# A two-layer encoder on one core: layer 0's up projection by Strassen's scheme, its first two products beside the top-k, index scores moved into the query projection

## The chip, the core and the metric

The kernel runs on one core of a Trainium2 chip. TensorE multiplies, VectorE, ScalarE and GpSimd do the elementwise work, and SyncE's queue issues all the DMAs. The metric is device time in microseconds (us) of one execution; the time before is the median of three runs. The profiler traced one more execution, and all rows here come from that one.

## What is computed

The input is 1024 tokens of width 1024, in float32. Cut to what matters:

```python
def reference(x, ...):                 # DEPTH = 2, x: (1, 1024, 1024)
    for i in range(DEPTH):
        h = rms_norm(x, norm_mix_g[i])
        x = x + (dsa_mixer(h, ...) if i == 0 else retention_mixer(h, ...))
        x = x + conv_ffn(rms_norm(x, norm_ffn_g[i]), f_w_up[i], f_conv_w[i], f_conv_b[i], f_w_down[i])

def dsa_mixer(h, w_in, q_g, k_g, iq_g, ik_g, w_out):    # 8 heads of 128, 8 index heads of 64
    ...                                # blocks of 128 queries
    rel = jax.nn.relu(jnp.einsum('bqhd,bsd->bqhs', qib, ki))
    score = jnp.einsum('bqhs,bqh->bqs', rel, wb)
    score = jnp.where(admissible[None], score, -jnp.inf)
    _, idx = lax.top_k(score, 256)     # attention over these keys only
    ...

def conv_ffn(h, w_up, conv_w, conv_b, w_down):          # D_FF = 2816
    u = h @ w_up                       # (1024, 5632)
    up = jnp.pad(u, ((0, 0), (2, 0), (0, 0)))
    u = sum(up[:, j:j + seq] * conv_w[j] for j in range(3)) + conv_b
    a, b = u[..., :D_FF], u[..., D_FF:]
    return (jax.nn.silu(a) * b) @ w_down
```

## The kernel before

Activations lie with the features on the partitions; tokens go in two halves of 512. Each float32 product is made as three products of a high and a low part (`mm3`, L137 to L139; `product`, L809, in Strassen's scheme). For every weight tile a DMA fetches `wraw`, ScalarE rounds it to `whi`, and VectorE or GpSimd subtracts to get `wlo` (`wprep`, L103); `plan_weights` lists the weights in order and says which `wlo` GpSimd makes.

Layer 0 goes like this. `in_proj` makes queries, keys and index queries of one token half. `indexer` makes the index scores of a query block: TensorE matmuls, ScalarE's relu, VectorE's weighted sum over heads (L397, L399). `topk` finds, for several blocks at once, the 256th largest score by a search over the 31 bits of a threshold: in each round VectorE counts the scores above the threshold, block by block (L420), and sets a bit by three small operations (L430 to L432); behind the last round it makes the mask, by a scan over the scores that equal the threshold (L434 to L443). `attention` goes block by block: logits, masking on VectorE (L501), exponential on ScalarE, scaling, transposes on TensorE (L529), product with the values. `out_proj` adds to `x` and sums the squares for the next norm (`square_sum`, L188), which `mean_square` (L194) adds up on TensorE.

The generators of these functions are interleaved by hand in `run`. Blocks 2 and 3 have their top-k beside `in_proj(1)`; then the attention of blocks 0 to 3 goes with the index scores of blocks 4 to 7, and their top-k, `steps(7)` a chunk, beside `ffn_half` of half 0: 22 chunks of 128 gate channels with 48 up matmuls each (two weight tiles by 24), `conv` on ScalarE and VectorE (L555 to L567), gating, and the down projection in groups of six chunks. Attention of blocks 4 to 7, `out_proj(1)`, layer 1's `retention(0)`, `ffn_half` of half 1 and `retention(1)` follow.

Layer 1's FFN (`ffn_whole`) is made for all 1024 tokens by Strassen's scheme: seven products of 12 matmuls of 512 columns stand in for the eight of a conventional 2 x 2 blocking. `B11` and `B21` are split from the first token half, `T1` to `T4` and `B22` need both halves. `ud` in DRAM takes the convolved outputs, `gate` loads them (`gin`), multiplies and splits, and the down projection works in groups of chunks listed in `DOWN`.

A scheduler with a model of the engines sets the final order of instructions on each engine; each engine then works in that order.

## Time and profile before

| what | us |
|---|---|
| median of three runs (2809.32 to 2809.56) | 2809.42 |
| the profiled execution | 2808.24 |
| its span, from first to last instruction | 2806.4 |
| TensorE busy | 2697.8 |
| VectorE busy | 1872.5 |
| ScalarE busy | 1110.8 |
| GpSimd busy | 379.7 |

The span is what the trace covers; the execution's own time lies 1.84 us above it. Busy times are sums over the span, in which several engines work at once, so an engine's share says nothing of which one is waited for in a given stretch.

### The profile page before, as it was taken

What the parts mean: (1) busy time and instruction counts of PE and PEld (TensorE: products, weight loads), DVE (VectorE), ACT (ScalarE), POOL (GpSimd) and SP (SyncE); (2) the same over time, 40 slices, a digit from 0 to 9 for tenths busy, and PEclk for the clock granted to TensorE, in tenths of its full rate; (3) what the DMA queues carried; (4) which work ended last, traced back from release to release, by engine and by line L of the source; (5) the groups of instructions that cost most, each with busy time, mean ns of one, the idle gap of its engine ahead of it and who ended that gap; (6) DMA issues with size and microseconds to landing.
All of it is one profiled execution on the core that took longest, in us unless ns stands there. A gap on an engine that the chain in (4) does not pass through costs nothing.

```text
span 2806.4 us, 31988 instructions
## 1 busy us (share of the span) xinstructions
PE 2697.8 (96%) x12152; PEld 2211.7 (79%) x12152; DVE 1872.5 (67%) x3028; ACT 1110.8 (40%) x1620; POOL 379.7 (14%) x247
## 2 busy tenths in 40 slices
PE   8987998998999999999999999999998999999999
PEld 6765776776887888888888888888886888888887
DVE  5798899999585444444767656445447977777632
ACT  6536533323464333334433334333333644544210
POOL 2555334343440000000000000000000000000000
PEclk9998999999999999999999999999999999999999
DMA  5221122222211222222332323222222322337612
GB/s 192 80 85 38 53 75 90 75 91 72 94 38 59 89 85 76 90 90 86 117 98 90 102 83 111 75 89 96 71 82 90 134 107 112 113 111 280 237 59 87
DMA packets 88170, 273.84 MB, mean 98 GB/s; under 512 B 9936, under 2 KB 11344, under 8 KB 88016
## 3 DMA queue, kind: packets, MB, share of 16 engines
q1 hardware_dynamic: 88016, 271.80, 28.7%
q8 instruction: 95, 1.56, 0.2%
q14 instruction: 59, 0.48, 0.1%
HBM read 234.54 MB, written 33.55 MB: 96 GB/s over the span
## 4 chain that ended last, share of the span: by engine, by line
PE 71%; DVE 9%; issue 2%; DMA 2%; POOL 1%; ACT 1%; SPq 0%; POOLq 0%; ACTq 0%; DVEq 0%
PE bank L137 19%; PE bank L139 19%; PE bank L138 19%; PE bank L809 13%; DVE scratch L420 3%; POOL wlo L103 1%; DVE t L561 1%; DMA gin<-ud 1%; DVE t L560 1%; PE bank L529 1%; DMA wraw<-in_wf_up 1%; DVE t L555 1%; DVE gl L584 0%; PE bank L766 0%; DMA wraw<-in_wf_dn 0%
## 5 line engine op out<-in xcount | busy, mean ns | idle before, releaser
L101 ACT ACTIVATE whi<-wraw 128x1024 fp32r<-128x1024 f32 (+3 forms) x324 | 324.5, 1003 | 676.6 <-PE bank L138 392.7
L137 PE MATMUL bank<-hh,whi 128*128 128x512 f32 (+2 forms) x1184 | 464.9, 393 | 17.9 <-ACT hh L148 11.6
L139 PE MATMUL bank<-hh,wlo 128*128 128x512 f32 (+2 forms) x1184 | 462.2, 391 | 11.0 <-POOL wlo L103 11.0
L138 PE MATMUL bank<-hl,whi 128*128 128x512 f32 (+2 forms) x1184 | 461.5, 390 | 3.5 <-DVE hl L149 3.4
L103 DVE TENSOR_TENSOR wlo<-wraw,whi 128x1024 fp32r<-128x1024 f32 (+3 forms) x227 | 266.6, 1175 | 240.8 <-ACT whi L101 238.0
L137 PEld LDWEIGHTS bank<-hh,whi 128*128 128x128 f32 (+1 forms) x1184 | 224.3, 189 | 67.2 <-ACT hh L148 13.2
L139 PEld LDWEIGHTS bank<-hh,wlo 128*128 128x128 f32 (+1 forms) x1184 | 224.0, 189 | 63.9 <-POOL wlo L103 16.1
L138 PEld LDWEIGHTS bank<-hl,whi 128*128 128x128 f32 (+1 forms) x1184 | 224.5, 190 | 51.8 <-DVE hl L149 4.3
L103 POOL TENSOR_TENSOR wlo<-wraw,whi 128x1024 fp32r<-128x1024 f32 (+2 forms) x97 | 220.0, 2271 | 309.7 <-ACT whi L101 298.7
L809 PE MATMUL bank<-T,whi 128*128 128x512 f32 x704 | 220.0, 394 | 10.4 <-ACT T L786 8.0
L138 PE MATMUL bank<-wlo,hh 128*128 128x512 f32 x512 | 199.3, 389 | 0.0
L139 PE MATMUL bank<-whi,hl 128*128 128x512 f32 x512 | 199.2, 389 | 0.0
L137 PE MATMUL bank<-whi,hh 128*128 128x512 f32 x512 | 198.8, 390 | 0.0
L420 DVE TENSOR_SCALAR_CACHE_REDUCE scratch<-sc,tkt 128x640 f16<-128x640 f32 (+1 forms) x192 | 180.5, 940 | 1.9
L786 ACT ACTIVATE whi<-wraw 128x1024 fp32r<-128x1024 f32 (+2 forms) x98 | 95.4, 973 | 198.7 <-PE bank L138 127.5
L809 PEld LDWEIGHTS bank<-T,whi 128*128 128x128 f32 x704 | 133.3, 189 | 41.2 <-ACT T L786 9.3
L809 PE MATMUL bank<-B,whi 128*128 128x512 f32 x528 | 162.8, 389 | 0.0
L787 DVE TENSOR_TENSOR wlo<-wraw,whi 128x1024 fp32r<-128x1024 f32 (+2 forms) x98 | 109.1, 1113 | 75.5 <-ACT whi L786 75.4
L139 PE MATMUL bank<-gh,wlo 128*128 128x512 f32 x352 | 139.7, 399 | 14.2 <-POOL wlo L103 13.9
L137 PE MATMUL bank<-gh,whi 128*128 128x512 f32 x352 | 138.5, 395 | 5.6 <-ACT whi L101 5.6
L138 PE MATMUL bank<-gl,whi 128*128 128x512 f32 x352 | 138.5, 394 | 0.0
L809 PE MATMUL bank<-T,wlo 128*128 128x512 f32 x352 | 137.5, 392 | 0.0
(251 smaller groups left out, 5376.9 us busy)
## 6 DMA issues: line engine op xcount, KB each, us to landing
wraw<-in_wf_up SPq DMA_DIRECT2D x135, 512.0 KB, 3.3
wraw<-in_wb_vg SPq DMA_DIRECT2D x64, 512.0 KB, 3.3
wraw<-in_wf_dn SPq DMA_DIRECT2D x72, 384.0 KB, 3.1
ud<-cu SPq DMA_DIRECT2D x44, 512.0 KB, 2.6
gin<-ud SPq DMA_DIRECT2D x44, 512.0 KB, 4.7
wraw<-in_wb_qk SPq DMA_DIRECT2D x32, 512.0 KB, 3.3
wraw<-in_wb_out SPq DMA_DIRECT2D x32, 512.0 KB, 3.3
wraw<-in_wa_in SPq DMA_DIRECT2D x26, 512.0 KB, 3.6
```

The costliest lines, as they stand in the source:

```text
L101: nc.scalar.activation(hi[:, :n], raw[:, :n], AF.Copy)
L103: eng.tensor_tensor(lo[:, :n], raw[:, :n], hi[:, :n].bitcast(F32), ALU.subtract)
L137: mm(ps, ah, bh, start=first, stop=False)
L138: mm(ps, ah, bl, start=False, stop=False)
L139: mm(ps, al, bh, start=False, stop=last)
L420: V.tensor_scalar(scratch[:, 0, :Ls[b]], scs[b], of(b), None, op0=op, op1=ALU.add, accum_out=cnt[:, b:b + 1])
L529: nc.tensor.transpose(pt[:, i * 128:(i + 1) * 128], lg[:, i, j * 128:(j + 1) * 128], self.ident)
L555: nc.vector.tensor_tensor(pn, ps, rbc, ALU.mult)
L560: nc.vector.scalar_tensor_tensor(u[:, 1:], ps[:, :511], w(1), u[:, 1:], op0=ALU.mult, op1=ALU.add)
L786: return (self.nc.scalar.activation(hi, raw, AF.Copy), self.nc.vector.tensor_tensor(lo, raw, hi.bitcast(F32), ALU.subtract))
L787: self.nc.vector.tensor_tensor(lo, raw, hi.bitcast(F32), ALU.subtract))
L809: self.nc.tensor.matmul(ps, u, v, start=first and k + i == 0, stop=k == 3 and i == 2, skip_group_check=not (first and last))
```

## The change

Layer 0's FFN is now made like layer 1's, for all tokens at once by Strassen's scheme. Two of the seven products, `A11 B11` and `A12 B21`, need the first token half alone: `first_products` makes them for 17 of the 22 chunks behind `out_proj(0)` and its norm, with three top-k steps at each of its yields, and stores them in DRAM (`pd`). The last five chunks follow `out_proj(1)`. `ffn_first` loads them and makes the five other products; for chunks from the fifth on, half of the conv is postponed to `gate` in `down`. The down projection is `down(0)`, with groups of 4, 6, 6 and 6 chunks, and `retention(0)` takes its split inputs from the last group.

The index scores of blocks 4 to 7 move into the query projection of `in_proj(1)` (`IDX_FROM`), the attention of blocks 0 to 3 goes with the start of the top-k of blocks 4 to 7, and so does `out_proj(0)` (`steps(5)` for each tile). The `halo` handling of the conv between token halves falls away, and buffers are laid out anew.

```diff
-DOWN = [(0, 6), (6, 6), (12, 6), (18, 4)]
-PRE = 4
+DOWN = (([(0, 4), (4, 6), (10, 6), (16, 6)], (14,)), ([(0, 6), (6, 6), (12, 6), (18, 4)], (0, 12)))
+PRE = (5, 4)
...
+            elif ph == "up":
+                seq += [(i["wf_up"][0, c], 1024, True) for c in range(*a)]
...
+    def first_products(self, cs, B):
+        def out(ps, c, i):
+            t = self.tmp()
+            nc.scalar.activation(t, ps, AF.Copy)
+            nc.sync.dma_start(self.pd[i][c], t)
+        last = None
+        for c in list(cs) + [None]:
+            cur = None
+            if c is not None:
+                hi, lo = self.weight()
+                a = self.bank()
+                self.product(a, (hi[:, :512], lo[:, :512]), B[0], True, False)
+                out(a, c, 0)
+                cur = c, a, (hi[:, 512:], lo[:, 512:])
+                yield
+            if last:
+                self.product(last[1], last[2], B[1], False, True)
+                out(last[1], last[0], 1)
+                yield
+            last = cur
...
+    def ffn_first(self, x, tt, s3):
+        chunk = self.normaliser(x1, C_GFFN, 1)
+        late = lambda c: c >= DOWN[0][0][0][1]
+        nxt = self.prep_b(0, 0, self.up_raw(0, 0), s3)
+        T1, T2, T4, B22, T3 = self.second_inputs(x0, x1, tt, chunk)
...
+        for c in range(NFF):
+            s1, s2, s3_, s4, a22 = nxt
...
+            nc.sync.dma_start(p1, self.pd[0][c])
+            nc.sync.dma_start(ca[:, :512], self.pd[1][c])
+            d = self.bank()
+            self.product(d, s1, T1, True, False)
+            p5 = self.tmp()
+            add(p5, d, p1)
+            if held:
+                finish(held)
+            a = self.bank()
+            self.product(a, s2, T2, True, False)
+            u2 = self.tmp()
+            add(u2, a, p1)
+            self.product(d, s4, B22, False, True)
+            add(ca[:, 512:], d, u2)
+            if c + 1 < NFF:
+                own = self.hp.tile([128, 2, 1024], F32R, tag="h", name="wb")
+                nxt = self.prep_b(0, c + 1, self.up_raw(0, c + 1), s3, (own[:, 0], own[:, 1]))
+            self.product(a, s3_, T3, False, False)
+            add(cb[:, 512:], a, p5)
+            held = c, a, a22, p1, cc
+        finish(held)
+        return self.down(0, tt, late)
...
         def gate(c):
...
+            nc.sync.dma_start(u, self.ud[l][1][c])
+            if late(c):
+                self.conv(l, NFF + c, u, v)
+                nc.sync.dma_start(u, self.ud[l][0][c])
+            else:
+                nc.sync.dma_start(v, self.ud[l][0][c])
+            add(u, u, v, ALU.mult)
...
     def run(self):
-                gens.append(self.topk([masks[2], masks[3]]))
-                att = self.attention(range(4), q0, masks, get_ot)
-                q1, qs1 = self.in_proj(1, *h1[:2], steps, lambda j, q: next(att) if j >= EARLY else None)
-                steps(100)
-                idx = (None for b in (4, 5, 6, 7) for _ in self.indexer(b, qs1, (b - 4) * 128, masks))
...
-                for i, _ in enumerate(att):
-                    if i % IDX_EVERY != 0:
-                        next(idx, None)
-                x[0] = self.out_proj(0, *ot, lambda: [next(idx, None) for _ in range(3)])
...
-                self.ffn_half(0, 0, x[0], self.ffn_part(0, 0, x[0], lag=2), steps=steps, early=early)
...
+                gens.append(self.topk([masks[2], masks[3]], scratch))
+                idx = []
+                def index(j, q, qs):
+                    if j == IDX_FROM:
+                        idx.append((None for b in (4, 5, 6, 7) for _ in self.indexer(b, qs, (b - 4) * 128, masks)))
+                    if j >= IDX_FROM:
+                        for _ in range(-(-32 // (8 - IDX_FROM))):
+                            next(idx[0], None)
+                q1, qs1 = self.in_proj(1, *h1[:2], steps, index)
+                steps(200)
+                gens.append(self.topk([masks[b] for b in (4, 5, 6, 7)], scratch))
+                for _ in self.attention(range(4), q0, masks, get_ot):
+                    steps(1)
+                x[0] = self.out_proj(0, *ot, lambda m: steps(5))
...
+                for _ in self.first_products(range(NFF - PRE[0]), B):
+                    steps(3)
+                steps(200)
+                for _ in self.attention(range(4, 8), q1, masks, get_ot):
+                    pass
+                B, ch = self.first_inputs(x[0])
+                x[1] = self.out_proj(1, *ot, lambda m: next(ch, None))
+                for i, _ in enumerate(self.first_products(range(NFF - PRE[0], NFF), B)):
+                    if i == 2:
+                        self.mean_square(1)
...
+                x, h = self.ffn_first(x, tt, s3)
```

What the scheduler makes of it on VectorE is seen at three places. The first is the attention of blocks 0 to 3; before, the rows of index scores of the later blocks (`sc<-...,wr`) stand among its masking (`lg<-bank,sc`) and scaling steps:

```order
L397 TENSOR_SCALAR sc<-t_2343,wr 128x512
L491 RECIPROCAL s_2312<-s_2297 128x1
L501 ISA lg_2091,s_2319<-bank,sc 128x384
L501 ISA s_2319 128x1
L397 TENSOR_SCALAR sc<-t_2349,wr 128x256
L506 SCALAR_TENSOR_TENSOR s_2321<-s_2319,sq 128x1
L491 RECIPROCAL s_2325<-s_2310 128x1
L491 RECIPROCAL s_2337<-s_2323 128x1
L501 ISA lg_2091,s_2374<-bank,sc 128x384
L501 ISA s_2374 128x1
```

After the change, counts of the top-k of blocks 4 to 7 (L405 now) stand there, with its small steps (`tkb`, `tkt`, `tks`) between them:

```order
L405 TENSOR_SCALAR scratch,tkc<-sc,tkt 128x896
L474 RECIPROCAL s_2485<-s_2470 128x1
L484 ISA lg_2375,s_2492<-bank,m_277 128x256
L484 ISA s_2492 128x1
L405 TENSOR_SCALAR scratch,tkc<-sc,tkt 128x1024
L489 SCALAR_TENSOR_TENSOR s_2494<-s_2492,sq 128x1
L415 TENSOR_SCALAR tkb<-tkc 128x4
L474 RECIPROCAL s_2498<-s_2483 128x1
L416 SCALAR_TENSOR_TENSOR tkt<-tkb,tks 128x4
L417 TENSOR_TENSOR tks<-tks,tkb 128x4
L405 TENSOR_SCALAR scratch,tkc<-sc,tkt 128x640
```

The scores have gone ahead of this place and about two thirds of the counting rounds have come to it and to `out_proj(0)` behind it. The second place is the top-k of blocks 4 to 7 at its middle; before, each count has conv steps of the FFN (`t<-...`) beside it:

```order
L420 TENSOR_SCALAR scratch,tkc<-sc,tkt 128x640
L560 SCALAR_TENSOR_TENSOR t_3734<-t_3732,cols,t_3734 128x511
L420 TENSOR_SCALAR scratch,tkc<-sc,tkt 128x768
L561 SCALAR_TENSOR_TENSOR t_3734<-t_3732,cols,t_3734 128x510
L555 TENSOR_TENSOR t_3740<-bank,rbc 128x512
L420 TENSOR_SCALAR scratch,tkc<-sc,tkt 128x896
L564 COPY halo<-t_3740 128x2
L560 SCALAR_TENSOR_TENSOR t_3742<-t_3740,cols,t_3742 128x511
L420 TENSOR_SCALAR scratch,tkc<-sc,tkt 128x1024
L561 SCALAR_TENSOR_TENSOR t_3742<-t_3740,cols,t_3742 128x510
L430 TENSOR_SCALAR tkb<-tkc 128x4
```

After, from the last split of `B21` on, VectorE has nothing but the top-k to the end of its 32 rounds:

```order
L405 TENSOR_SCALAR scratch,tkc<-sc,tkt 128x640
L405 TENSOR_SCALAR scratch,tkc<-sc,tkt 128x768
L405 TENSOR_SCALAR scratch,tkc<-sc,tkt 128x896
L405 TENSOR_SCALAR scratch,tkc<-sc,tkt 128x1024
L415 TENSOR_SCALAR tkb<-tkc 128x4
L416 SCALAR_TENSOR_TENSOR tkt<-tkb,tks 128x4
L417 TENSOR_TENSOR tks<-tks,tkb 128x4
L405 TENSOR_SCALAR scratch,tkc<-sc,tkt 128x640
L405 TENSOR_SCALAR scratch,tkc<-sc,tkt 128x768
L405 TENSOR_SCALAR scratch,tkc<-sc,tkt 128x896
L405 TENSOR_SCALAR scratch,tkc<-sc,tkt 128x1024
```

The conv steps are gone from beside it. The third place is the up projection of layer 0; before, here for the second token half, a chunk is conv steps of 512 columns, the gating (`t<-t,t`, `gl`) and two splits of weights:

```order
L555 TENSOR_TENSOR t_10915<-bank,rbc 128x512
L197 TENSOR_SCALAR msq<-bank 128x4
L103 TENSOR_TENSOR wlo<-wraw,whi 128x1024
L560 SCALAR_TENSOR_TENSOR t_10917<-t_10915,cols,t_10917 128x511
L561 SCALAR_TENSOR_TENSOR t_10917<-t_10915,cols,t_10917 128x510
L566 SCALAR_TENSOR_TENSOR t_10917<-halo,cols,t_10917 128x2
L567 SCALAR_TENSOR_TENSOR t_10917<-halo,cols,t_10917 128x1
L581 TENSOR_TENSOR t_10917<-t_10908,t_10917 128x512
L584 TENSOR_TENSOR gl<-t_10917,gh 128x512
L555 TENSOR_TENSOR t_10988<-bank,rbc 128x512
L103 TENSOR_TENSOR wlo<-wraw,whi 128x1024
```

After, one chunk of `ffn_first` is sums of weights (`wraw`, `t<-wraw`), sums of products from the banks, three splits and two conv steps over all tokens:

```order
L742 TENSOR_TENSOR t_7093<-wraw 128x512
L742 TENSOR_TENSOR wraw<-wraw 128x512
L742 TENSOR_TENSOR t_7039<-bank,t_7023 128x512
L742 TENSOR_TENSOR wraw<-wraw 128x512 x2
L742 TENSOR_TENSOR cu<-bank,t_6925 128x512
L742 TENSOR_TENSOR t_7073<-bank,t_7023 128x512
L709 TENSOR_TENSOR wlo<-wraw,whi 128x1024
L709 TENSOR_TENSOR wb<-wraw,wb 128x1024
L742 TENSOR_TENSOR cu<-bank,t_7073 128x512
L742 TENSOR_TENSOR cu<-bank,t_7039 128x512
L835 SCALAR_TENSOR_TENSOR cu<-cu,cols 128x1023
L709 TENSOR_TENSOR wlo_7105<-t_7093,whi_7104 128x512
L836 SCALAR_TENSOR_TENSOR cu<-cu,cols 128x1022
```

The multiplication of the two halves of the gate has moved from here to the down projection.

## Rows read from the trace of the kernel before

**Rows 1.** The page, part 1: busy us (share of span) xinstructions of each engine.

```profile
PE 2697.8 (96%) x12152; PEld 2211.7 (79%) x12152; DVE 1872.5 (67%) x3028; ACT 1110.8 (40%) x1620; POOL 379.7 (14%) x247
```

**Rows 2.** Stretches: length; busy (xinstructions) of PE, PEld, DVE, ACT, POOL; clock, DMA.

```profile
106.20:341.20 235.00, 199.48 (x908) 157.81 (x907) 210.32 (x495) 121.30 (x240) 113.22 (x75) 0.93 0.21 64
...
365.50:690.00 324.50, 294.15 (x1247) 233.04 (x1245) 321.52 (x554) 107.50 (x137) 129.25 (x55) 0.99 0.26 82
...
762.40:918.10 155.70, 148.49 (x767) 123.92 (x766) 109.63 (x272) 86.55 (x147) 34.66 (x32) 0.98 0.17 58
918.10:1351.80 433.70, 431.98 (x1985) 359.81 (x1984) 206.40 (x306) 149.72 (x233) 10.63 (x17) 1.00 0.27 90
...
2148.00:2192.70 44.70, 34.29 (x130) 25.48 (x129) 42.65 (x54) 24.00 (x30) 0.00 (x0) 0.85 0.17 59
2192.70:2545.00 352.30, 352.29 (x1555) 291.69 (x1555) 268.29 (x307) 178.07 (x209) 0.00 (x0) 1.00 0.32 117
```

**Rows 3.** Waits of the engines in 106.2 to 690: us, times, longest.

```profile
DVE x L546 <- PE bank L139: 7.5, 2, 5.7
...
PE bank L391 <- DVE s L501: 6.8, 1, 6.8
```

**Rows 4.** VectorE by line and shape, 340 to 690: xcount, busy us, mean ns.

```profile
L420 DVE TENSOR_SCALAR_CACHE_REDUCE scratch<-sc,tkt 128x1024 f16<-128x1024 f32 x32 | 40.7, 1271 | 0.3
...
L420 DVE TENSOR_SCALAR_CACHE_REDUCE scratch<-sc,tkt 128x640 f16<-128x640 f32 x32 | 27.9, 873 | 0.0
...
L430 DVE TENSOR_SCALAR tkb<-tkc 128x4 int32<-128x4 f32 x31 | 13.9, 450 | 0.3
...
L431 DVE SCALAR_TENSOR_TENSOR tkt<-tkb,tks 128x4 int32<-128x4 int32 x31 | 7.1, 229 | 0.4
L432 DVE TENSOR_TENSOR tks<-tks,tkb 128x4 int32<-128x4 int32 x31 | 6.0, 195 | 0.5
...
L434 DVE TENSOR_SCALAR tkn<-tkc 128x4 f32<-128x4 f32 x1 | 2.4, 2354 | 0.0
...
L438 DVE TENSOR_TENSOR_SCAN scratch<-scratch 128x1024 f16<-128x1024 f16 x1 | 2.3, 2275 | 0.0
```

**Rows 5.** Timeline of VectorE: start us, length us, one instruction a row.

```profile
111.25 1.97 DVE L430 TENSOR_SCALAR tkb<-tkc 128x2 int32<-128x2 f32 x1
...
116.01 0.17 DVE L430 TENSOR_SCALAR tkb<-tkc 128x2 int32<-128x2 f32 x1
...
361.29 0.87 DVE L420 TENSOR_SCALAR_CACHE_REDUCE scratch<-sc,tkt 128x640 f16<-128x640 f32 x1
...
365.77 0.17 DVE L430 TENSOR_SCALAR tkb<-tkc 128x4 int32<-128x4 f32 x1
...
560.51 0.68 DVE L555 TENSOR_TENSOR t<-bank,rbc 128x512 f32<-128x512 f32 x1
561.11 0.15 DVE L432 TENSOR_TENSOR tks<-tks,tkb 128x4 int32<-128x4 int32 x1
```

**Rows 6.** TensorE's timeline: attention of blocks 4 to 7; retention 1.

```profile
762.42 0.60 PE L529 MATMUL bank<-kon,lg 128*128 128x128 f32 x4
...
1708.16 1.16 PE L194 MATMUL bank<-ones,acc 128*128 128x128 f32 x8 [0.23 <-DVE acc L188]
```

**Rows 7.** Timeline of TensorE at layer 1's first product with T.

```profile
2155.62 0.80 PE L809 MATMUL bank<-T,whi 128*128 128x512 f32 x1 [6.27 <-ACT T L786]
```

**Rows 8.** VectorE by line and shape, 2192.7 to 2545 (layer 1's up products).

```profile
L787 DVE TENSOR_TENSOR wlo<-wraw,whi 128x1024 fp32r<-128x1024 f32 x57 | 69.7, 1223 | 70.0 <-ACT whi L786 70.0
L821 DVE TENSOR_TENSOR cu<-bank,t 128x512 f32<-128x512 f32 x76 | 50.4, 685 | 11.0 <-PE bank L809 11.0
L911 DVE SCALAR_TENSOR_TENSOR cu<-cu,cols 128x1023 f32<-128x1023 f32 x39 | 49.9, 1280 | 0.0
```

**Rows 9.** DMA traffic, 2545 to 2600 (layer 1's up projection ends).

```profile
DMA packets 6472, 18.74 MB, mean 341 GB/s; under 512 B 719, under 2 KB 719, under 8 KB 6468
```

**Rows 10.** GpSimd by line and shape, 106 to 690.

```profile
L103 POOL TENSOR_TENSOR wlo<-wraw,whi 128x1024 fp32r<-128x1024 f32 x59 | 148.2, 2513 | 208.1 <-ACT whi L101 204.6 <-PE bank L392 3.4
```

More of the change, by code (lines that the diff above doesn't have):

```diff
@@ L50 @@
 LAG = 3
-EARLY = 4
-IDX_EVERY = 2
-IDX_FIRST = 4
+IDX_FROM = 3
 class Prog:
@@ L345, in in_proj @@
             pq = self.proj_T(hh, hl)
+            steps((2, 6)[half])
+            also(j, q, qs)
             sq = squares(pq)
@@ new lines, in first_inputs, with chunks @@
+    def first_inputs(self, x0):
+        B = [self.hp.tile([128, 2, 4, 512], F32R, tag="h", name=n) for n in ("B11", "B21")]
+        def chunks():
+            for t, o in zip(B, (0, 4)):
+                for k in (0, 2):
+                    self.split(self.two(t, 0, k), self.two(t, 1, k), self.two(x0, o + k))
+                    yield
+        return B, chunks()
+    def first_products(self, cs, B):
+        nc = self.nc
+        def out(ps, c, i):
[15 more added lines that the diff above has]
+                out(last[1], last[0], 1)
+                yield
+            last = cur
@@ L887, in ffn_whole, with second_inputs @@
+    def second_inputs(self, x0, x1, tt, chunk):
+        two, add = self.two, self.add
+        T1, T2, T4, B22, T3 = [tt.tile([128, 2, 4, 512], F32R, tag="T", name=n) for n in ("T1", "T2", "T4", "B22", "T3")]
         for k in (0, 2):
@@ new lines, in run @@
+                steps(200)
[3 more added lines that the diff above has]
+                x[0] = self.out_proj(0, *ot, lambda m: steps(5))
+                ot.clear()
+                self.mean_square(0)
+                chunk = self.normaliser(x[0], C_GFFN, 0)
+                for k in range(8):
+                    chunk(k)
+                B, ch = self.first_inputs(x[0])
```

407 lines of the change are left out of this document (188 added, 219 removed).

## The prediction

> **What bounds the kernel now.** I read the page first. TensorE is busy 96% of the span and VectorE 67% [rows 1]. These are averages, so the table of stretches comes next [rows 2]. From 762.4 us to the end TensorE hardly rests: in 2192.7 to 2545 it is busy 352.29 of 352.30 us with 1555 matmuls, which gives 0.2266 us for each, at a granted clock of 1.00 (the 2.4 GHz level). Removing matmuls there shortens the run one for one. From 106.2 to 690 it is otherwise: VectorE is busy 210.32 of 235.00 us to 341.2 and 321.52 of 324.50 us from 365.5, TensorE 199.48 and 294.15. Here both are nearly full at once: the top-k of blocks 4 to 7 lies beside 325 us of TensorE's FFN matmuls. What leaves that stage on TensorE is gained only as far as VectorE doesn't take its place.
>
> **Matmuls.** The order lists 264 fewer 512-column matmuls: the conventional up projection of layer 0 has 44 x 2 x 24 = 2112, Strassen's seven products of 12 in 22 chunks are 1848. At 0.2266 us that is 59.8 us. This would be the whole gain if every stage stayed full of TensorE work.
>
> **The stage from 106.2 us to the first products.** VectorE's order there (up to the row of the last `B21` split) holds all that it did until 341.2, and further:
> - 22 of the 32 counting rounds of the second top-k. A round has four counts, 0.873 us for 640 columns, 1.271 for 1024 and by width 1.006 and 1.138 between, and three small steps, 0.450, 0.229 and 0.195 us [rows 4]. 22 counts of 1024 columns, 21 of each other width and 20 sets of small steps are 28.0 + 63.4 + 17.5 = 108.9 us; its start is a small step from counts like the one of 2.354 us [rows 4], 2.4.
> - three sums of squares, two additions of `out_proj` and eight products of the normaliser, at 0.685 us, a 512-column operation's price: 8.9; two 1024-column splits of `B11` at 1.223, 2.4 [rows 8]; less five `hl` splits, at least 3.4.
> - less overlap. An instruction that doesn't need the one ahead starts before that has ended: one of 0.68 us at 560.51 is followed 0.60 us later [rows 5]. Dependent ones don't. For some 190 added instructions I take 10 off, 0.05 each, an estimate.
>
> Together 109 us. VectorE idled 235.0 - 210.3 = 24.7 us there. 7.5 us of that were additions waiting for TensorE's work of `out_proj` [rows 3]. With counts to fill them I take 5 of 24.7; bounds 0 and 24.7. Start of the first products: 106.2 + 210.3 + 109 + 5 = 430.5 us. TensorE's work in the stage (199 us before) is far less, so VectorE sets this.
>
> **First products against the rest of the top-k.** Seventeen chunks by 24 matmuls are 408 x 0.2266 = 92.5 us, so TensorE is done at 523. VectorE meanwhile has the last 44 counts, their small steps, and the top-k's end. A round without other work took 4.5 us from its first count (361.29) to its first small step (365.77), and 0.5 for three steps of 0.17: 5.0 [rows 5]. Eleven are 55; the small steps at their mean instead of 0.17 each add 0.36 a round, 4. The end is a small step of 2.354 and for each block a scan, 2.275 us for 1024 columns [rows 4], and four more passes that I take at a count's price each: by width (3328 columns in all) 3.25 x (2.275 + 4 x 1.271) = 24, and 26 with the small step. That is 85 us, to 516, some us more if steps stretch: nearly a tie. The blocks' first probabilities then need a score mask, an exponential and a scaling before a transpose. Nothing shows this chain by itself; the nearest row is TensorE's wait of 6.8 us for the masking step of blocks 0 to 3 [rows 3]. Bounds 0 and 10, I take 7: first transposes at 530, where before they stood at 762.42 [rows 6].
>
> **From there.** All terms are TensorE's.
> - 762.42 to 918.1 is 155.7 us and held, by the order, 24 retention matmuls (5.4) and 10 FFN matmuls (2.3) that are now elsewhere [rows 2]: 148.0, to 678.
> - the last five chunks' first products: 120 x 0.2266 = 27.2, to 705.
> - the wait for `T1`: in layer 1 the first product with `T` starts 6.3 us late, followed by gaps and slower matmuls. 130 matmuls there take 44.7 us instead of 29.5, so 15.2 are lost [rows 2, 7]. Here, by the order, some 8 us of products stand after the normaliser's broadcast instead of 6, so I take 13, bounds 8 and 18: 718.
> - the five other products: 5 x 12 x 22 = 1320, 299.1 and 2 for the clock: 1019.
> - the down projection: 22 x 8 x 2 x 3 = 1056, 239.3, and 4 for its first loads: 1263.
> - retention 0: 433.7 us in [rows 2], less two FFN chunks' 48 matmuls that stood in it (10.9), plus its own first 24 (5.4), plus 1: 1692.
> - the rest as from the mean square at 1708.2 to the end, 1098.2, plus 5.4 for the one retention chunk that stood ahead of it [rows 6]: 2795.6.
>
> Span 2795.6 instead of 2806.4. The profiled execution took 2808.24, 1.84 over its span, and the median of the runs is 1.18 over that: **2798 us**, 11 us less. Of the 59.8 us some 49 are lost, almost all of it in the stage to 530: VectorE's work to the end of the top-k can't shrink, it only stops being spread over FFN matmuls.
>
> **What is costed at nothing, and its cover.** Conv work moves out of the top-k stage. In the new loop VectorE has per chunk ten 512-column operations (0.685), two 1024-column splits (1.223) and two conv steps (1.280) [rows 8]: 6.9 + 2.4 + 2.6 = 11.9 us, TensorE 60 x 0.2266 = 13.6. The 1.7 us is the cover; it is thinner than in layer 1, where VectorE is busy 268 of 352. Bounds 0 and 1 us a chunk, 22 us; I take 0. The postponed half of the conv adds a ScalarE step and 2.56 us of VectorE to each later gate of the down projection, where a group of six chunks has 65 us of matmuls. The first group's loads are its open part: in layer 1 this stretch moved 18.74 MB at 341 GB/s and TensorE still got its operands [rows 9]. Mine has 16.75 MB (gate inputs, 16 loads of `xo`, weights), 49 us at that rate, against 43.5 us of first-group matmuls. Bounds 0 and 15, I take 4. Storing the early products (44 of 256 KB) and `xd[0]` goes to SP's queue among weight loads at 64 to 82 GB/s of traffic in the stage's rows: nothing.
>
> **GpSimd beside the small steps.** It makes `wlo` of the 17 chunks, 2.513 us each [rows 10], just beside the top-k's tail. In the trace `L430` took 1.97 us where it takes 0.17 a round later, while counts keep their length [rows 5]; the mean of the three steps, 0.87 us a round beside as many GpSimd operations, already holds such cases, and I use it. The Trainium skill, "SBUF — State Buffer", section "Who interferes with whom", says that VectorE and GpSimd share one pair of ports under an exclusive lock, which operations with two inputs from SBUF and plain `tensor_scalar` can meet, the form that writes its accumulator not. The trace agrees: small steps stretch, counts don't. By that rule at its worst each of the 17 operations would hold VectorE for its whole length, 43 us.
>
> **Rivals.**
> - *Slower: VectorE's stage keeps its idle time.* If all 24.7 us stay, since scores and softmax still wait for ScalarE in program order, 20 us come on top: 2818. For it: the stretch's row. Against: counts wait for nothing but each other, so they fill gaps. It decides from 17 us over my sum on.
> - *Slower: GpSimd blocks the small steps.* If each of the 17 `wlo` costs a small step 1.97 - 0.17 = 1.8 us, the top-k ends at 516 + 31 = 547 instead of TensorE at 523: 2822. If each blocks for its 2.513 us, 559: 2834. For it the 1.97 us; against it that the mean of 0.450 for that step was measured beside the same operations.
> - *Slower by the up loop.* At 11.9 of 13.6 us, VectorE, in order behind TensorE's banks, may cost 1 us a chunk: 2820. From 0.77 us a chunk on the run is slower by over 0.2%.
> - *No change that can be measured.* 17 of the stage's 24.7 us of idle time stay, 12 more than I take: 2810. TensorE then rests as much longer in the stage as the matmuls had given, 60 us.
> - *More gained.* No idle time (5), small steps at 0.17 us each, 0.36 less a round (8 in the first 22), no chain (7): 2778.
>
> **Chances.** About 0.2%, 5.6 us, is what a measurement of this kernel tells from no change, so faster ends at 2803.8 and slower begins at 2815. My forecast (2788 to 2804) 0.42, more gained 0.15, no change 0.20, idle time kept 0.10, GpSimd 0.04, up loop 0.09. Faster 0.57, same 0.20, slower 0.23. The range 2772 to 2826 leaves out the far ends of the slow cases and the tip of the fast one, under 2 in 10.
>
> **What would show it.** In the table of stretches of the changed kernel: VectorE busy over 95% from 106 to 520 and TensorE well under 70% until the first products; these start at 425 to 440; the first transposes of blocks 4 to 7 at 520 to 540; then TensorE over 98% to the end but for one gap before the first `T` product; five-product loop 299 to 305 us; last down group without waits for `gin`. First products beginning after 450, or the loop taking over 315 us, would make me wrong.

## The result and the profile after

The changed kernel took 2786.65 us (median of four runs, 2782.56 to 2787.80) against 2809.37; the ratio is 0.9916 (0.9899 to 0.9934). In a second series, `e9_changed_again` below, it was 0.9925 (0.9913 to 0.9938). So the change gains 21 to 23 us, where 11 were forecast: the direction and the range held, the size was off by half. The profiled execution is the fastest of the four runs, with 2782.56 us and a span of 2780.8; the second series' profile had 2784.5, so a few microseconds of what follows are scatter.

The page of the changed kernel, part 1, which answers to [rows 1]:

```profile
span 2780.8 us, 31488 instructions
...
PE 2654.3 (95%) x11888; PEld 2175.0 (78%) x11888; DVE 1881.0 (68%) x2928; ACT 1090.9 (39%) x1546; POOL 264.9 (10%) x193
```

TensorE's busy time fell by 43.5 us and not by 59.8, and its idle time rose from 108.6 to 126.5 us. In the stage from 106.2 us it works in pieces, at a mean granted clock of 0.83 where [rows 2] had 0.93, and its matmuls take longer there. The table of stretches of the changed kernel, cut where its order changes (first products, attention of blocks 4 to 7, late products, making of `T`, five-product loop, first down group, the rest of down, retention 0); columns as in [rows 2]:

```profile
106.20:415.80 309.60, 233.06 (x942) 177.26 (x940) 299.94 (x738) 131.34 (x246) 118.45 (x79) 0.83 0.19 59
...
415.80:513.50 97.70, 97.14 (x429) 80.66 (x429) 93.78 (x164) 36.51 (x53) 37.97 (x15) 0.98 0.52 170
513.50:660.00 146.50, 143.41 (x748) 118.87 (x749) 108.77 (x264) 85.79 (x145) 41.93 (x36) 1.00 0.20 66
660.00:688.00 28.00, 23.87 (x114) 19.66 (x112) 11.40 (x17) 10.39 (x15) 5.80 (x3) 1.00 0.46 150
688.00:715.00 27.00, 18.64 (x58) 12.27 (x59) 27.00 (x35) 13.87 (x17) 0.00 (x0) 0.81 0.22 74
715.00:1001.50 286.50, 283.75 (x1253) 234.45 (x1251) 239.66 (x302) 109.61 (x111) 0.00 (x0) 1.00 0.60 197
1001.50:1045.00 43.50, 41.65 (x174) 33.64 (x175) 33.84 (x39) 14.45 (x16) 0.00 (x0) 0.96 0.82 289
1045.00:1249.00 204.00, 202.51 (x893) 167.04 (x892) 139.91 (x153) 65.21 (x72) 0.00 (x0) 1.00 0.41 128
1249.00:1683.80 434.80, 432.90 (x1989) 360.55 (x1988) 210.12 (x318) 150.93 (x237) 11.62 (x18) 1.00 0.29 92
```

The single rows at which these marks stand, from TensorE's timeline: the first product with `B11`, the one from which they run without a gap, the first transpose of block 4, the first product with `T`, the first matmul of the down projection, and its last one with retention behind it.

```profile
410.76 1.65 PE L731 MATMUL bank<-B,whi 128*128 128x512 f32 x3 [3.22 <-ACT B L708]
415.85 0.80 PE L731 MATMUL bank<-B,whi 128*128 128x512 f32 x1 [3.44 <-DVE B L709]
...
513.51 0.33 PE L512 MATMUL bank<-kon,lg 128*128 128x128 f32 x1 [0.52 <-POOL lg L475]
...
688.07 0.50 PE L731 MATMUL bank<-T,whi 128*128 128x512 f32 x1 [4.20 <-ACT T L708]
...
1001.47 1.94 PE L123 MATMUL bank<-g,whi 128*128 128x512 f32 x6 [2.75 <-ACT g L708]
...
1249.61 0.39 PE L125 MATMUL bank<-g,wlo 128*128 128x512 f32 x1
1249.84 0.39 PE L123 MATMUL bank<-hh,whi 128*128 128x512 f32 x1
```

Against the sum: the first products run from 415.85 (forecast 430.5), the first transposes come at 513.51 (530), late products end at 683.9 (705), the loop ends at 998.7 with TensorE waiting 2.75 us for the first gate (1019), and retention 0 starts at 1249.8 (1263). From there to the end 1531.0 us are left, forecast 1532.8. Nearly all of the 14.8 us by which the span beats the forecast is there at 415.85; behind that point the terms are off by 1 to 8 us each, some up and some down, and these errors cancel.

VectorE in that stage, by line and shape (106.2 to 415.8), for [rows 4] and [rows 5]:

```profile
L385 DVE SCALAR_TENSOR_TENSOR sc<-t,wr,sc 128x512 f32<-128x512 f32 x28 | 29.7, 1093 | 0.1
L405 DVE TENSOR_SCALAR_CACHE_REDUCE scratch<-sc,tkt 128x1024 f16<-128x1024 f32 x20 | 25.5, 1274 | 0.1
...
L415 DVE TENSOR_SCALAR tkb<-tkc 128x2 int32<-128x2 f32 x31 | 17.2, 555 | 0.7
...
L416 DVE SCALAR_TENSOR_TENSOR tkt<-tkb,tks 128x2 int32<-128x2 int32 x31 | 12.3, 398 | 1.0
...
L416 DVE SCALAR_TENSOR_TENSOR tkt<-tkb,tks 128x4 int32<-128x4 int32 x20 | 6.0, 298 | 0.3
...
L415 DVE TENSOR_SCALAR tkb<-tkc 128x4 int32<-128x4 f32 x20 | 4.4, 218 | 0.1
...
L417 DVE TENSOR_TENSOR tks<-tks,tkb 128x4 int32<-128x4 int32 x20 | 4.0, 201 | 0.3
```

### The profile page after: what moved, and what is told of

Same layout as the page of the kernel before. It is cut to its first block, busy times and chain, and to the rows that moved or that the text cites. A ratio compares the mean times of both kernels' runs of the same rounds, so it can differ in the third digit from the quotient of the medians.

```text
span 2780.8 us, 31488 instructions
## 1 busy us (share of the span) xinstructions
PE 2654.3 (95%) x11888; PEld 2175.0 (78%) x11888; DVE 1881.0 (68%) x2928; ACT 1090.9 (39%) x1546; POOL 264.9 (10%) x193
## 4 chain that ended last, share of the span: by engine, by line
PE 77%; DVE 4%; DMA 2%; ACT 1%; issue 1%; POOL 0%; SPq 0%; DVEq 0%; ACTq 0%
PE bank L731 28%; PE bank L123 16%; PE bank L125 16%; PE bank L124 16%; PE bank L512 1%; DMA gin<-ud 1%; DMA wraw<-in_wf_up 1%; DVE T L709 1%; DVE xo L742 1%; DVE wlo L709 1%; PE bank L688 0%; DVE t L742 0%; DVE x L717 0%; DMA ud<-cu 0%; DVE gin L742 0%
## 5 line engine op out<-in xcount | busy, mean ns | idle before, releaser
L87 ACT ACTIVATE whi<-wraw 128x1024 fp32r<-128x1024 f32 (+1 forms) x194 | 204.9, 1056 | 510.3 <-PE bank L124 263.0
L731 PE MATMUL bank<-T,whi 128*128 128x512 f32 x1072 | 336.8, 395 | 21.9 <-ACT T L708 14.8
L731 PE MATMUL bank<-B,whi 128*128 128x512 f32 x1056 | 326.4, 392 | 7.7 <-DVE B L709 4.0
L89 DVE TENSOR_TENSOR wlo<-wraw,whi 128x1024 fp32r<-128x1024 f32 (+1 forms) x151 | 184.6, 1224 | 209.0 <-ACT whi L87 207.9
L124 PE MATMUL bank<-g,whi 128*128 128x512 f32 x704 | 273.6, 389 | 0.0
L125 PE MATMUL bank<-g,wlo 128*128 128x512 f32 x704 | 272.1, 389 | 0.5 <-DVE wlo L709 0.5
L123 PE MATMUL bank<-g,whi 128*128 128x512 f32 x704 | 265.5, 390 | 5.6 <-ACT g L708 4.6
L731 PEld LDWEIGHTS bank<-T,whi 128*128 128x128 f32 x1072 | 203.9, 190 | 70.4 <-ACT T L708 16.5
L731 PEld LDWEIGHTS bank<-B,whi 128*128 128x128 f32 x1056 | 198.8, 189 | 50.5 <-DVE B L709 5.0
L731 PE MATMUL bank<-B,wlo 128*128 128x512 f32 x528 | 204.1, 390 | 0.0
L123 PE MATMUL bank<-hh,whi 128*128 128x512 f32 (+2 forms) x480 | 188.6, 393 | 11.3 <-ACT hh L134 8.9
L124 PE MATMUL bank<-hl,whi 128*128 128x512 f32 (+2 forms) x480 | 186.5, 389 | 0.1
L125 PE MATMUL bank<-hh,wlo 128*128 128x512 f32 (+2 forms) x480 | 186.0, 388 | 0.0
L405 DVE TENSOR_SCALAR_CACHE_REDUCE scratch<-sc,tkt 128x640 f16<-128x640 f32 (+1 forms) x192 | 180.7, 941 | 2.4
```

Source lines behind the costliest of these rows:

```text
L87: nc.scalar.activation(hi[:, :n], raw[:, :n], AF.Copy)
L89: eng.tensor_tensor(lo[:, :n], raw[:, :n], hi[:, :n].bitcast(F32), ALU.subtract)
L123: mm(ps, ah, bh, start=first, stop=False)
L124: mm(ps, ah, bl, start=False, stop=False)
L125: mm(ps, al, bh, start=False, stop=last)
L405: V.tensor_scalar(scratch[:, 0, :Ls[b]], scs[b], of(b), None, op0=op, op1=ALU.add, accum_out=cnt[:, b:b + 1])
```

## The experiments

Each ratio is against runs of the kernel before on the same chip, and the changed kernel's own stands at 0.9916 and 0.9925; 0.001 is 2.8 us. Two experiments shorten the top-k's search, which changes its threshold; this is said where it applies.

**Each half of the change alone.** `e1_scores_late` is the changed kernel with scores and top-k of blocks 4 to 7 where they were before, and with four top-k steps instead of three at each yield of the first products; `e2_scores_early_only` is the kernel before with only these moved, and with buffers and numbers of steps to suit. The edits are cut to what matters:

```diff
 e1, in run():
-                q1, qs1 = self.in_proj(1, *h1[:2], steps, index)
+                q1, qs1 = self.in_proj(1, *h1[:2], steps)
...
-                gens.append(self.topk([masks[b] for b in (4, 5, 6, 7)], scratch))
-                for _ in self.attention(range(4), q0, masks, get_ot):
-                    steps(1)
-                x[0] = self.out_proj(0, *ot, lambda m: steps(5))
+                for i, _ in enumerate(self.attention(range(4), q0, masks, get_ot)):
+                    if i % 2 != 0:
+                        next(idx, None)
+                x[0] = self.out_proj(0, *ot, lambda m: [next(idx, None) for _ in range(3)])
+                gens.append(self.topk([masks[b] for b in (4, 5, 6, 7)], scratch))
 e2, in run() of the kernel before: the reverse, and steps(4) for steps(7) in ffn()
```

> Strassen's scheme as in the change, but the index scores of blocks 4 to 7 stay among the attention of blocks 0 to 3, and their top-k starts only with the first products. Theory (VectorE's total work up to the end of that top-k sets the time, and the change pays because it starts the top-k early): first products start near 372 us as the FFN did before, 92 us of them end near 465, but 32 counting rounds at 4.8 us and 28 us of mask steps last until about 550, so TensorE waits some 85 us; first transposes of blocks 4 to 7 near 555 instead of 513.5; time 2820 to 2835. Rival (the 264 matmuls saved are the gain, the order of the rest is worth little): 2782 to 2795.

> The kernel before with only the new order of the index scores and the early start of the top-k of blocks 4 to 7; layer 0's FFN stays conventional, in halves. Theory: VectorE's stage lasts until about 410, then 1584 FFN matmuls of half 0 run at TensorE's pace, 359 us, with TensorE's gaps there gone: first transposes at 768 to 775 instead of 762; time 2812 to 2822, no gain by the order alone. Rival (the order itself removes VectorE's waits and is the gain): below 2800.

Measured: e1 2822.54 us, ratio 1.0055 (1.0040 to 1.0070); e2 2833.29 us, 1.0094 (1.0079 to 1.0110). Both halves alone are slower than the kernel before, by 15 and 26 us; together they gain 22. In e1 the first products start at 363.5 us, but TensorE's timeline has a hole ahead of the first transposes, since VectorE is not done with the top-k. The transposes come 21 us earlier than the 555 that I expected:

```profile
363.52 1.65 PE L731 MATMUL bank<-B,whi 128*128 128x512 f32 x3 [3.22 <-ACT B L708]
...
534.49 0.48 PE L512 MATMUL bank<-kon,lg 128*128 128x128 f32 x1 [67.91 <-POOL lg L475]
```

In e2, VectorE is full until the top-k ends near 570 us while TensorE is held to 152 of 162 us, and the FFN then goes on at TensorE's pace; the transposes come at 790 us, 28 later than [rows 6]. My estimate was 768 to 775: it left out that the conv's VectorE work still lies beside the last rounds.

```profile
408.00:570.00 162.00, 151.96 (x646) 122.69 (x646) 160.94 (x266) 51.89 (x64) 65.52 (x28) 0.96 0.24 78
570.00:790.00 220.00, 217.38 (x948) 177.50 (x948) 139.58 (x183) 83.85 (x113) 96.67 (x50) 0.99 0.29 91
```

So the early top-k pays because there are few FFN matmuls left to put beside it, and the two-product FFN pays because most of the top-k is done by then.

**VectorE's work in the first stage.** In `e3_first_topk_short` ten bit rounds of the first top-k are left out.

```diff
-        for k in range(30, -1, -1):
+        for k in range(30, 9 if B == 2 else -1, -1):
```

> The changed kernel, with 10 of the 31 bit rounds of the top-k of blocks 2 and 3 left out (its threshold is coarser). This takes about 26 us of VectorE work out of the stage from 106 us to the first products and nothing else. Theory (VectorE sets that stage): first products 18 to 26 us earlier than 415.8, time 2760 to 2769. Rival (waits for ScalarE, GpSimd and TensorE set it): less than 8 us earlier, time above 2778.

Measured: 2781.84 us, ratio 0.9911 (0.9896 to 0.9926). Neither theory's numbers: the products run from 405.7, 10 us earlier. VectorE's busy time there fell from 299.94 to 281.68 us and its idle time rose from 9.7 to 17.8 (the row below). It is nearly the bound, no more: with less to count it waits for ScalarE's relu of the index scores, 8.0 us in 13 waits, of which the changed kernel has none. And of 6.7 us that the first product with `T` came earlier (681.35), half was gone at the loop's end.

```profile
106.20:405.70 299.50, 229.66 (x937) 175.72 (x935) 281.68 (x659) 129.84 (x244) 117.51 (x78) 0.83 0.19 61
```

**GpSimd beside the top-k's end.** `e4_wlo_vector` gives the 17 early low parts to VectorE.

```diff
-                seq += [(i["wf_up"][0, c], 1024, True) for c in range(*a)]
+                seq += [(i["wf_up"][0, c], 1024, a[0] > 0) for c in range(*a)]
```

> The changed kernel with the low parts of the 17 early weight tiles made by VectorE instead of GpSimd: 17 x 1.22 = 21 us more VectorE work beside the end of the top-k. Theory (VectorE's work sets the first transposes and GpSimd costs it little): transposes 15 to 21 us later than 513.5, time 2800 to 2809. Rival (GpSimd's operations block VectorE for their length, so that VectorE gets back what it takes over): within 5 us of the changed kernel, 2782 to 2792.

Measured: 2790.30 us, ratio 0.9940 (0.9923 to 0.9956), some 4 to 7 us slower: a time in the rival's range, but with the transposes 9.7 us later, at 523.17, which lies between the two. Three timelines show what GpSimd costs at the masks of blocks 4 and 5. VectorE's in the changed kernel:

```profile
481.17 2.58 DVE L428 TENSOR_SCALAR sc<-sc 128x640 f32<-128x640 f32 x1
...
486.10 2.97 DVE L425 SCALAR_TENSOR_TENSOR scratch<-scratch,tkn 128x768 f16<-128x768 f16 x1
```

GpSimd's timeline in the changed kernel at the same place:

```profile
480.46 2.94 POOL L89 TENSOR_TENSOR wlo<-wraw,whi 128x1024 fp32r<-128x1024 f32 x1 [2.58 <-ACT whi L87]
485.04 3.22 POOL L89 TENSOR_TENSOR wlo<-wraw,whi 128x1024 fp32r<-128x1024 f32 x1 [1.64 <-PE bank L731]
```

And VectorE's timeline of e4, at the first of these two steps:

```profile
499.76 0.49 DVE L428 TENSOR_SCALAR sc<-sc 128x640 f32<-128x640 f32 x1
```

`L428` on 640 columns takes 0.49 us alone and 2.58 beside GpSimd: it begins inside the GpSimd operation that runs from 480.46 to 483.40 and ends just after it. `L425` at 486.10 does the same with the operation up to 488.26. Four such steps cost 8.1 us, the first of the small steps (`L415`, 0.296 against 0.167 in e4) 1.4 more, and the one that ends the search (`L419`, 1.225 against 0.161) 1.1: 10.6 us for 17 GpSimd operations. The expectation of e11 below still has 9.5, without `L419`. Counts keep their lengths. So do the four scans here, but none of them begins well inside a GpSimd operation; one that does is seen in e6 below. VectorE needs 17 x 1.22 = 20.8 us to make these parts itself. This is the exclusive lock of the Trainium skill, "SBUF — State Buffer", section "Who interferes with whom"; the trace agrees with its kinds of operations, and the 10.6 us are far from the 43 us of its worst case, since most GpSimd operations fall beside counts.

**The norm of the second half, and the first weights.** `e5_early_norm` issues the broadcast behind its mean square.

```diff
                     if i == 2:
                         self.mean_square(1)
+                    if i == 3:
+                        chunk = self.normaliser(x[1], C_GFFN, 1)
 and ffn_first() takes chunk instead of making it
```

> The changed kernel, with the broadcast of the second token half's norm put right behind its mean square instead of behind the last first products. In the changed kernel the inverse roots are ready at 662.4 us, their broadcast stands 13 us later in TensorE's order, and VectorE and ScalarE have little to do until then; the products with T then run slowly until about 713. Theory (the late broadcast is what is lost there, some 17 us in all): broadcast 8 to 10 us earlier, time 6 to 11 us below the changed kernel, 2776 to 2781. Rival (the loads and splits of the first weights for the other products are what is late): within 3 us of it.

Measured: 2786.50 us, 0.9930 (0.9918 to 0.9943), no gain, as the rival had it. But its reason is not shown. The first product with `T` stays at 688.0, where it now waits only 0.90 us, for the high part of a weight, instead of 4.20; the late products ahead of it end 3 us later than in the first profile. The loop ends at 997.1, 1.6 us earlier than in the first profile and 4.9 earlier than in the second. This lead is lost in the down projection, where TensorE waits for a later gate:

```profile
1071.07 2.50 PE L123 MATMUL bank<-g,whi 128*128 128x512 f32 x5 [4.50 <-ACT g L708]
```

Ahead of it ScalarE waits up to 6.4 us for the gates' loads (`gin`), in the changed kernel there at most 2.9. `e10_early_weights` adds a slot of their own for the first weights:

```diff
+        r = tt.tile([128, 2, 1024], F32, tag="T", name="wraw")
+        for i in range(2):
+            nc.sync.dma_start(r[:, i], self.ins["wf_up"][0, i * NFF])
-        nxt = self.prep_b(0, 0, self.up_raw(0, 0), s3)
+        nxt = self.prep_b(0, 0, r[:, 0], s3, None, r[:, 1])
```

> The changed kernel once more, as the base for the two kernels beside it on the same chip: 2783 to 2788, and first products, first transposes and the first product with T within 3 us of 415.8, 513.5 and 688.1.

> The kernel with the early broadcast, and the two weight tiles of the first of the five-product chunks loaded into a slot of their own (that of T3, which is made last) instead of behind the early products' tiles. With the early broadcast alone the first product with T still started at 688, now held up by weights: VectorE had no weight to work on until about 676. Theory (normalising, weights and the splits of T share VectorE from 676 to 713, so both the norm and the weights must be early for either to pay): the first product with T no later than 686, TensorE's idle time to 715 down by 6 to 12 us, time 6 to 12 us below the changed kernel. Rival (VectorE's splits alone fill that time): within 3 us of it.

Measured beside each other: e9 2787.03 us, 0.9925 (0.9913 to 0.9938), with its marks 2 to 3 us behind the first profile's; e10 2780.85 us, 0.9904 (0.9891 to 0.9918), 6 us better. The first product with `T` follows the last late one without a gap, at 683.93. But the loop ends at 996.3, only 0.8 us earlier than in e5, and the gate at 1067.53 is waited for 1.2 us and not 4.5. VectorE's waits for weight loads from 655 to 1003 us are 17 us in the changed kernel, 2 in e5 and 7 in e10. So the two profiles don't show that it is the early weights that gain the 6 us.

**The tie, and the loop's cover.**

```diff
 e6_few_rounds
-        for k in range(30, -1, -1):
+        for k in range(30, -1 if B == 2 else 4, -1):
 e7_no_late
-        late = lambda c: c >= DOWN[0][0][0][1]
+        late = lambda c: False
 e8_pre2
-PRE = (5, 4)
+PRE = (2, 4)
```

> The changed kernel without the last 5 bit rounds of the top-k of blocks 4 to 7 (a coarser threshold): 25 us of VectorE work less beside the first products. Theory (top-k and first products end in a tie, so that TensorE's 97 us of first products hold the attention back as well): first transposes at most 6 us earlier than 513.5, time 2779 to 2787. Rival (the top-k alone sets them): 20 us or more earlier, time below 2768.

> The changed kernel with both halves of the conv in the up loop for all chunks: 18 x 2.56 = 46 us of VectorE work come back into a loop in which VectorE is busy 240 of 286 us, and leave the down projection. Theory (the loop's cover is thin): the five-product loop 5 to 20 us longer, time 2791 to 2806. Rival (TensorE stays ahead all the same): within 3 us, 2784 to 2790.

> The changed kernel with 20 chunks of first products beside the top-k and 2 behind the second output projection, instead of 17 and 5. The matmuls are the same. Theory (17 is a tie with the top-k, and the late ones cover the making of T): first transposes 13 to 16 us later, 16 us fewer late products but as much more waiting for T, time 2796 to 2806. Rival (only the sum of matmuls counts): 2783 to 2790.

Measured: e6 2783.10 us, 0.9918 (0.9905 to 0.9932): the top-k of blocks 4 to 7, five rounds short, ends 20 us earlier, the first transposes come at 515.1, no earlier, and TensorE's first products hold the attention as long as the top-k did. e7 2796.70 us, 0.9969 (0.9957 to 0.9981): the first product of the down projection comes at 1020 instead of 1001, which makes the loop, from the first product with `T` to there, some 17 us longer; the lighter gates give about a third of it back. e8 2786.74 us, 0.9933 (0.9917 to 0.9948): transposes 15 us later, 16 us fewer late products, and only 9 us of waiting for `T` at 690.49; here the rival was right, and 17 is no special number.

The trace of e6 also has a scan that begins inside a GpSimd operation, on VectorE and on GpSimd:

```profile
466.97 4.10 DVE L423 TENSOR_TENSOR_SCAN scratch<-scratch 128x896 f16<-128x896 f16 x1
...
466.38 2.82 POOL L89 TENSOR_TENSOR wlo<-wraw,whi 128x1024 fp32r<-128x1024 f32 x1 [2.50 <-ACT whi L87]
```

It takes 4.10 us, where this scan takes 2.03 in the changed kernel and 2.02 in e4: scans are blocked as well when GpSimd comes first.

**GpSimd ahead of the first products.** `e11_wlo_stage_vector` moves the low parts of the second input projection and the first output projection to VectorE, `e15_before_wlo_vector` does it in the kernel before.

```diff
-                seq += [(i["wa_in"][c], 1024, a == 1) for c in [8, 9, 10, 11, 12] + list(range(8))]
+                seq += [(i["wa_in"][c], 1024, False) for c in [8, 9, 10, 11, 12] + list(range(8))]
-                seq += [(i["wa_out"][m], 1024, a == 0) for m in range(8)]
+                seq += [(i["wa_out"][m], 1024, False) for m in range(8)]
```

> The changed kernel with the low parts of the second input projection's and the first output projection's weights made by VectorE instead of GpSimd: 21 x 1.22 = 26 us more VectorE work in the stage ahead of the first products, 21 GpSimd operations less. In that stage the small steps and scores of VectorE stretch by some 40 us in all over their lengths without GpSimd. Theory (most of this stretching comes from those GpSimd operations, as in the top-k's end, where 17 of them cost 9.5 us): VectorE gets back 12 to 26 us of the 26, first products 0 to 14 us later than 415.8, time 0 to 14 us above the changed kernel. Rival (the stretching has other causes): 20 to 30 us later.

> The kernel before, with the low parts of the second input projection's and the first output projection's weights on VectorE instead of GpSimd, and nothing else. Its VectorE was busy 210 of 235 us in that stage, with small steps at three times their length without GpSimd. Theory (GpSimd's operations hold up VectorE there in the kernel before as well): FFN start 10 to 25 us earlier than 358, time 2785 to 2800. Rival (only the changed order makes VectorE the bound there): within 4 us of the kernel before.

Measured: e11 2781.52 us, 0.9907 (0.9892 to 0.9922); e15 2791.76 us, 0.9940 (0.9927 to 0.9954). Both theories for e11 had the wrong sign: the first products run from 390.5, 25 us earlier. Its stretch, VectorE's groups in it, and GpSimd's that remain:

```profile
106.20:390.50 284.30, 224.79 (x939) 172.59 (x937) 273.10 (x720) 131.24 (x244) 73.73 (x59) 0.84 0.20 64
...
L89 DVE TENSOR_TENSOR wlo<-wraw,whi 128x1024 fp32r<-128x1024 f32 x19 | 24.0, 1261 | 2.7 <-ACT whi L87 2.6
...
L385 DVE SCALAR_TENSOR_TENSOR sc<-t,wr,sc 128x512 f32<-128x512 f32 x28 | 20.5, 748 | 0.0
...
L415 DVE TENSOR_SCALAR tkb<-tkc 128x2 int32<-128x2 f32 x31 | 8.6, 278 | 0.3
...
L416 DVE SCALAR_TENSOR_TENSOR tkt<-tkb,tks 128x2 int32<-128x2 int32 x31 | 6.0, 193 | 0.8
...
L89 POOL TENSOR_TENSOR wlo<-wraw,whi 128x1024 fp32r<-128x1024 f32 x3 | 7.2, 2384 | 28.8 <-DVE tkt L416 22.7 <-ACT whi L87 6.1
```

From 346.0 us of VectorE's summed lengths in the changed kernel 321.4 are left: 24.0 more for `wlo` (`L89`), 17 less for three to four counting rounds that now stand behind the first products, and some 31 less because other operations shrink on balance: scores (`L385`) from 1.093 to 0.748 us, `L415` on two columns from 0.555 to 0.278, `L416` from 0.398 to 0.193. So these GpSimd operations of 2.41 us cost VectorE 1.5 to 1.6 us each, more than the 1.26 that it needs to do them. The top-k ends 7 us earlier, and by the order block 4's masking now stands ahead of block 7's mask: transposes at 497.66. In e15 the FFN's mean square moves from 356.8 to 334.2 and the run gains 17 us, so this was so before the change as well. The two rows, of the kernel before and of e15:

```profile
356.76 0.53 PE L194 MATMUL bank<-ones,acc 128*128 128x128 f32 x1
...
334.22 0.38 PE L194 MATMUL bank<-ones,acc 128*128 128x128 f32 x1
```

e11's first product with `T` is 14 to 18 us earlier (673.81), but the loop takes 324 us instead of 313, and the run gains 5.5. VectorE waits for weight loads in it, 12.7 us in six places, against 2.2 in the changed kernel; 14.9 us more lie just ahead of the first product with `T`, as 15.3 do in the changed kernel. One of the six:

```profile
786.20 0.69 DVE L742 TENSOR_TENSOR t<-wraw 128x512 f32<-128x512 f32 x1 [4.14 <-DMA wraw<-in_wf_up]
```

**Together.** `e12_both` has the early norm, the early weights and the stage's low parts on VectorE; `e13_both_pre3` also 19 early chunks, `e14_both_late2` postpones half of the conv from the third chunk on.

```diff
 e13
-PRE = (5, 4)
+PRE = (3, 4)
 e14
-        late = lambda c: c >= DOWN[0][0][0][1]
+        late = lambda c: c >= 2
```

> Early broadcast, early weights and the stage's low parts on VectorE together. Alone they gave 6 and 5.5 us; with the low parts on VectorE the first product with T came 15 us earlier, and the up loop took 324 instead of 313 us, waiting on splits and weight loads in its first eight chunks. Theory (the loop's first chunks are paced by VectorE, with both halves of the conv in the first four, so a lead at T is partly lost there): first product with T 19 to 23 us earlier than in the changed kernel's 688 to 691, loop 320 to 328 us, time 2774 to 2780. Rival (the gains add up): 2768 to 2773.

> The same, with 19 chunks of first products beside the top-k instead of 17 (with the low parts on VectorE, TensorE idled 9.6 us ahead of the first transposes). Theory (11 us of late products fill that gap): first transposes 0 to 3 us later than with 17, first product with T 6 to 10 us earlier; but the loop's first chunks take most of it, so time 0 to 5 us below the one with 17. Rival (TensorE's idle time there is what counts): 8 to 11 us below it.

> As with both, but half of the conv is postponed from the third chunk on instead of the fifth: 5.1 us of VectorE work less in the loop's first chunks, and as much more in the first gates of the down projection. Theory (VectorE paces those chunks): loop 3 to 8 us shorter, of which the first down group gives back 0 to 5; time 0 to 6 us below the one with both. Rival (weight loads behind stores in the queue pace them): loop within 2 us, time 0 to 5 us above it.

Measured: e12 2765.52 us, 0.9847 (0.9833 to 0.9860), the best version, 43 us below the kernel before and some 21 below the changed one: more than the two gains added. `T` starts at 668.97 and the loop takes 315 us, with 3.6 us of waits for weight loads. So the rival came nearer, though the time lies below its range too, and the loss in e11's loop went with late weights. That it was not VectorE's two conv halves in the first chunks is what e14 points to: 2777.34 us, 0.9889 (0.9875 to 0.9902), the loop only 2 us shorter, but the down projection 12 us longer to the start of retention 0, with gates that TensorE waits for 7.2 and 5.3 us. e13 took 2774.12 us, 0.9875 (0.9862 to 0.9889), 9 us above e12 where both theories had it below: transposes 6 us later, and 5.3 us of waiting for `T`, for which the two chunks less are missed now.

TensorE's timeline of e12, at the first product with `T` and the first of the down projection:

```profile
668.97 0.39 PE L731 MATMUL bank<-T,whi 128*128 128x512 f32 x1
...
984.14 2.93 PE L123 MATMUL bank<-g,whi 128*128 128x512 f32 x6 [2.89 <-ACT g L708]
```

In e14 the first product of the down projection comes at 981.59, after a wait of 2.76 us; the gate that is 7.2 us late follows 18 us behind it, where e12 waits 1.96:

```profile
999.98 2.93 PE L123 MATMUL bank<-g,whi 128*128 128x512 f32 x6 [7.20 <-ACT g L708]
```

## Why the prediction came out half as large

**What bounds the stage: right in kind.** VectorE is busy 299.94 of 309.60 us ahead of the first products, TensorE 233.06: 97% and 75%. Over 95% was forecast for VectorE, and well under 70% for TensorE, whose work took 34 us more than the 199 of before at a mean granted clock of 0.83 instead of 0.93. e1 and e2 show that the change pays only through how the top-k and the matmuls are laid beside each other, the point from which the sum took its loss of 49 of 59.8 us.

**The term that was mis-sized** is "The stage from 106.2 us to the first products": 109 us of added VectorE work and 5 us of idle time. Measured are 299.94 - 210.32 = 89.6 and 309.60 - 299.94 = 9.7, together 14.7 us less, which is the whole difference of the spans. Of the 19.4 us less work, about 3 are small steps of the top-k (0.72 us a round instead of 0.87), 3 its start (0.4 us instead of 2.4) and one count that stands later than I put it, some 3 more overlap, and about 10 the balance of operations that were there before: most got shorter, some 20 us in all, such as `L416` on two columns from 0.496 to 0.398, while index scores on 512 columns grew from 0.826 to 1.093, 7.5 us in all. The step behind it: lengths that are a mean over undisturbed operations and blocked ones were taken as fixed prices. e11 and e15 show how much they hang on GpSimd's place: without 21 of its operations about 31 us of VectorE's lengths are gone. GpSimd was busy 113 us in the stage before the change and 118 after it, over 75 us more of the stage; that the added work met less of it for this reason is argued, not shown. The rule weighed in the prediction was used as a threat for the 17 operations behind the first products, where it cost 10.6 us; the 21 ahead of them cost three times as much, in the kernel before too, and the sum carried that along unseen.

**First products against the top-k: right.** A tie, as e6 (transposes no earlier without five rounds) and e4 (transposes 9.7 us later with the top-k's end 17 us later) show. The chain of first probabilities, 7 us, was hidden, and TensorE's first products took 97 us instead of 92.5: the transposes stand at 513.5 where 523 + 7 = 530 were forecast, 16.5 earlier, of which the stage gave 14.7.

**The wait for T: right in kind, short in size.** 13 and 2 us were forecast between the late products and the steady loop; 683.9 to 998.7 less 299.1 makes 15.7. Its cause is told in part: the wait at the first product with `T` is 4.20 us in the changed kernel, 0.90 with the early norm (e5) and none with early weights as well (e10), but shortening this wait alone gained nothing (e5).

**The up loop: right.** No cost showed (283.75 of 286.5 us busy); e7, 17 us longer with 46 us more VectorE work, shows that the cover was thin and needed the postponing. **Down:** 12 us above its matmuls from the loop's end (251.1 us) instead of 4, within the bounds of 0 and 15; 2.75 and 1.85 of it are waits for the first gates. **Attention of blocks 4 to 7 and late products:** 170.4 us for 175.2. **Retention 0 and the rest:** 1531.0 for 1532.8. That the down projection's 8 us more don't show in the total is luck: the terms around it came out as much shorter.

**The rivals.** "More gained" named the right direction, with the small steps and the idle time as its cause; the small steps gave a part, the chain was hidden as it said, idle time went the other way, and it put 2778 on a chance of 0.15. The measured 2786.65 lies between it and the forecast's own 2788 to 2804. Idle time kept, GpSimd at its worst, a starving loop: none of them came.

What stays open: what gains e10's 6 us. Why e3's and e11's lead at `T` is lost to weight loads in just those loops and not in e12's was seen in the waits, not traced to the single buffer or queue entry that makes them late.

## What to carry to other kernels

Two changes that each make a kernel slower can be a gain together when one frees the engine that the other fills; time them together and apart. When work is moved from one stretch to another, take its price from its undisturbed rows and count what the neighbours add as a term of its own, because the neighbours change with the move. A lead at one mark is not yet time saved: in e5 and e14 gates of the down projection took it back. Before giving elementwise work to a second engine "for nothing", add up how much longer the first engine's other operations become beside it.

## What the runs showed of the hardware

A GpSimd subtraction of two 128x1024 tiles (2.41 us) that was already running held up some of VectorE's operations until it had ended: a `tensor_scalar` went from 0.49 to 2.58 us, a step with two inputs from 1.02 to 2.97, a scan on 896 columns from 2.03 to 4.10 (e6). Where a scan or a step with two inputs had begun first, it kept its length and the GpSimd operation grew, to 2.9 to 3.8 us. Over the first stage this came to 1.5 to 1.6 us of VectorE for each GpSimd operation, more than the 1.22 to 1.26 us that VectorE needs for the same subtraction. Counts (0.871 to 0.873 us on 640 columns) were the same with GpSimd and without.
